# A whole-network kernel: the router's top two from one comparison of all pairs, and another order at the experts' end

## The chip, the cores and the metric

The kernel runs on 1 core of one Trainium2 chip. The metric is the device time in microseconds of one execution. The kernel before takes 2173.37 us, the median of 3 runs (2173.23 to 2174.28).

A core has TensorE (PE, matmuls, with its weight loads shown as PEld), VectorE (DVE), ScalarE (ACT), GpSimd (POOL), and SyncE (SP), from which most DMAs are issued here. Each engine works through its own instructions in the order in which they were written down, and waits on semaphores for the others.

## The reference

256 tokens of width 1024 go through two blocks. The first has two layers of SwiGLU, a token mixer of three attentions, and SwiGLU. The second has two layers of attention followed by a mixture of experts; this is the part that the change touches:

```python
def second_block(x, c, ...):
    silu_c = jax.nn.silu(c)
    for i in range(DEPTH):                                  # 2
        mod = silu_c @ ada_w[i] + ada_b[i]
        sh1, sc1, g1, sh2, sc2, g2 = [m[:, None, :] for m in jnp.split(mod, 6, axis=-1)]
        h = rms_norm_2(x, norm_mix_g[i]) * (1.0 + sc1) + sh1
        y = diff_attention(h, ...) if i % 2 == 0 else chunked_attention(h, ...)
        x = x + g1 * y
        h = rms_norm_2(x, norm_ffn_g[i]) * (1.0 + sc2) + sh2
        x = x + g2 * grouped_moe(h, router_w, router_bias, moe_w_gate[i], moe_w_up[i], moe_w_down[i])
    return x

def grouped_moe(h, router_w, router_bias, w_gate, w_up, w_down):
    scores = jax.nn.sigmoid(t @ router_w)                   # t: 256 tokens; 16 experts
    sel = scores + router_bias
    grp = sel.reshape(-1, N_GROUPS, E_PER_GROUP)            # 4 groups of 4
    group_score = lax.top_k(grp, TOP_K)[0].sum(-1)          # the two best of each group
    _, g_idx = lax.top_k(group_score, TOPK_GROUPS)          # the best group
    masked = jnp.where(expert_mask, sel, NEG_INF)
    _, e_idx = lax.top_k(masked, TOP_K)                     # the two best experts in it
    w = jnp.take_along_axis(scores, e_idx, axis=1)
    w = w / jnp.sum(w, axis=-1, keepdims=True)
    for e in range(N_EXPERTS):
        he = jax.nn.silu(t @ w_gate[e]) * (t @ w_up[e])
        out = out + gates[:, e:e + 1] * (he @ w_down[e])
```

## The kernel before

The tokens lie in two tiles of 128 partitions, `x[:, t]`, and each is worked on in halves of 512 columns. The program is one straight sequence of ten stages: 0 to 5 are block one; 6 is the differential attention, 7 the experts, 8 the chunked attention, 9 the experts again.

**Weights.** All weights come as pieces of 128 x 1024 through one stream, issued on SP (L81) into a shared ring of slots; a piece can be loaded when a slot is free. Outside the experts every product is made in three matmuls (L332 to L334): ACT casts the piece into a high part `hi` (L122), DVE subtracts it from the piece for the low part `lo` (L127), and PE multiplies hi by hi, hi by lo and lo by hi. The experts' weights are used as they come, unsplit (L1592 gate and up, L1611 and L1672 down).

**The plan.** `plan` writes down the order in which the stream's pieces are used. Among a stage's weights it mixes the rows of the modulation matrices (ada items) that the next stages need. An ada item brings no matmul: DVE multiplies it into an accumulator `aacc` (L420, L422); the last of a group leads to sums by PE (L440), a copy `zs` by ACT (L442), transposes by PE, and two small DVE steps `mc` (L454, L456). Before, the ada items of a stage are spread over all its units from the first on. In the experts' stage 7 the first four units of stage 8 are already loaded (`EARLY`, `mine`).

**Steps at the side.** Small steps wait in a queue and are let out between matmuls by `tick`; `flush` in the attention's output projection (`proj_halves`) runs what is left, one after the other.

**Router** (`moe`, L1842 on). Squares on ACT, a mean and a power (`rpow`: DVE L554, POOL L557) give each tile's norm factor `r`; PE makes the logits from transposed raw `x` (L1876), and `z` (L1880) applies the factor to them. `norm` scales x to `xn` (DVE, L1884), `high` and `low` split `xn` for the gather (L1887, L1891). After the Sigmoid (L1939) DVE adds the bias (`sel`) and finds the top two of each group by two calls of `first_hit` of five steps each (L1567 to L1574) and a step that masks the first hit, then the best group by a third call. `eb` marks the two experts; PE makes prefix sums of it (L1963 on), which with an offset per expert (`pz`) give each token's two slots (`pc`, `slot`, `sl`). One-hot rows of the slots (L1982, L1983) are the matrices by which PE gathers the tokens for the first chunk of four experts (L1717); ACT and DVE scale what was gathered into `hg` (L1720, L1722), and the experts' matmuls begin.

**End of the experts** (`pairs` and `end`). When the last pair of experts is done, each half of `x` is updated (L1636), squared (L2051), and each tile gets its factor by `rpow`; `normed` (L594) scales tile 0, PE transposes it, and `trans` (L596 on) applies the modulation (`hf`, L616) and splits it into `hT` (L617, L610) for the first product of stage 8. `fills(2)` takes two pieces of the stream in this place, one behind each tile's factor.

**Stage 8** (`attn2`, L1358 on). Heads go in two groups; each makes q, k (normalised on DVE, `qs` L1350, transposed on PE, scaled on ACT, `qk` L1355) and v (copied by ACT, L1396). Softmax units: scores on PE (L850, L853), bias and maximum on DVE (L872, L876), eight exponentials on ACT (L879), normalised (L887, L890), transposed on PE, multiplied by v (L913). They run between the projections' matmuls.

Of the kernel before, what the change touches and what calls it, by code (L numbers as in the profile page):

```python
# [21 lines left out]
P = 128  # L22
# [23 lines left out]
for _name, _w in (  # L46
    ("cc", 16), ("adab", 144), ("npre", 48), ("gpost", 48), ("adab2", 96), ("nmix", 16), ("nffn", 16),
    ("aqg", 1), ("akg", 1), ("bqg", 1), ("bkg", 1), ("subln", 1), ("router", 128), ("rbias", 16),
    ("cosp", 32), ("sinp", 32), ("cosm", 64), ("sinm", 64), ("code", 4), ("eoff", 32), ("coff", 4),
):  # L50
    CV[_name] = (_n, _w)
    _n += _w
# [135 lines left out]
class Net:  # L188
# [309 lines left out]
    def plan(self, stages):  # L498
# [23 lines left out]
        for st in stages:  # L522
            wl, mine, early = wls[st], early, []

            nxt = self.next.get(st)
            ahead = {len(wl) - 4 * (EARLY - i): wls[nxt][i] for i in range(EARLY)} if st > 6 and st % 2 and nxt else {}
            if st == stages[0]:
                k = 4 if st == 0 else 0
                for it in wl[:k] + first[n:]:
                    self.stream.add(*it)  # L530
                wl = wl[k:]
            must = sum(1 for s, late, _ in queue if s == st or (s == st + 1 and not late))
            n = max(must, min(len(queue), ADA_PER[st]))
            al, queue = queue[:n], queue[n:]
            span = ADA_SPAN[st] * len(wl)
            done = 0
            for i, it in enumerate(wl):
                while done < n and done * span <= i * n:
                    self.stream.add(*al[done][2])
                    done += 1  # L540
                if i in ahead:
                    early.append(self.stream.add(*ahead[i], later=True))
                if i < len(mine):
                    self.stream.uses.append(mine[i])
                else:
                    self.stream.add(*it)
            assert done == n
# [1029 lines left out]
    def pairs(self, hg, gsl, row, OHT, ahead, done, end):  # L1577
# [111 lines left out]
        fill = self.stream.fills(2)  # L1689
# [6 lines left out]
        end(0, 1, fill[:1])  # L1696
        end(1, 0)
        S(7, 1, 1)
        for f in fill[1:]:
            f()  # L1700
# [142 lines left out]
    def moe(self, st, pre, rest):  # L1843
# [42 lines left out]
        def high(t, q):  # L1886
            nc.scalar.copy(xs[0, t][:, q * 512:(q + 1) * 512], xn[t, q])  # L1887
# [39 lines left out]
        power(1)  # L1927
        low(0, 0)
# [33 lines left out]
        pp = self.ps("acc")
        nc.tensor.matmul(pp[:, 0:16], self.ustrictb, eb[:, :16], start=True, stop=True)  # L1963
        nc.tensor.matmul(pp[:, 16:32], self.ustrictb, eb[:, 16:], start=True, stop=False)
        nc.tensor.matmul(pp[:, 16:32], self.onesb, eb[:, :16], start=False, stop=True)
        nc.tensor.matmul(pp[:, 32:48], self.onesb, eb[:, :16], start=True, stop=False)
        nc.tensor.matmul(pp[:, 32:48], self.onesb, eb[:, 16:], start=False, stop=True)
        low(1, 0)
        pz = self.sm(32, name="pz", bufs=1)
        nc.vector.tensor_tensor(out=pz, in0=pp[:, :32], in1=self.col("eoff"), op=ALU.add)  # L1970
        pc = self.sm(64, name="pc", bufs=1)
        nc.vector.tensor_tensor(out=pc.rearrange("p (c n) -> p c n", c=2), in0=ch.rearrange("p (c n) -> p c n", c=2),
                                in1=pz[:, None, :].broadcast_to([P, 2, 32]), op=ALU.mult)
# [4 lines left out]
        nc.vector.tensor_tensor(out=v3(sl, 4), in0=slot[:, None, :].broadcast_to([P, 4, 4]), in1=self.col("coff")[:, :, None].broadcast_to([P, 4, 4]), op=ALU.subtract)  # L1978

        def hot(oh, t, c):  # L1980
            o = self.t2(name="oh1")
            nc.vector.tensor_scalar(out=o[:, :256], in0=self.iota, scalar1=sl[:, 4 * c + t:4 * c + t + 1], scalar2=None, op0=ALU.is_equal)  # L1982
            nc.vector.scalar_tensor_tensor(out=oh[:, t * 256:(t + 1) * 256], in0=self.iota, scalar=sl[:, 4 * c + 2 + t:4 * c + 3 + t], in1=o[:, :256],  # L1983
                                           op0=ALU.is_equal, op1=ALU.add)
# [4 lines left out]
        next(chunks[0])  # L1989
        low(1, 1)  # L1990
# [51 lines left out]
        def end(t, h, fills=()):  # L2042
# [20 lines left out]
        return nxt, lambda n: lambda: nxt and self.normed(nxt, 1, rs[1])  # L2063
# [19 lines left out]
def prep(inputs):  # L2083
# [7 lines left out]
    def tables(n_rot):  # L2091
# [16 lines left out]
        "eoff": rep(np.tile(1024 * np.arange(16), 2).astype(np.float32)), "coff": rep(4096 * np.arange(4).astype(np.float32)),  # L2108
    }
# [66 lines left out]
```

## Time and profile before

| | before |
|---|---|
| median of 3 runs | 2173.37 us (2173.23 to 2174.28) |
| the profiled execution | 2171.94 us, its span 2170.2 us |
| PE, DVE, ACT, POOL busy | 94%, 63%, 42%, 4% of the span |
| HBM read | 590.00 MB, 273 GB/s over the span |
| stages 6 to 9 end near | 1530, 1787, 1922, 2170 us |

The profiled execution is one of its own; its span is what the views show, and the 1.74 us around it are outside them. All durations in the rows are from it. A busy share is a mean over stages that have different limits: where a stage waits for weights, the DMA share is near 1 and PE's matmuls (0.60 us in the experts) follow the stream; where it doesn't, the gaps in PE's row count. A row of the timeline gives the start in us from the span's start, the duration, engine, line, operation, output and inputs, and in brackets how long the engine stood idle before it and what ended that.

### The profile page before, as it was taken

To read this page: it belongs to the slowest core of one execution; us is meant where nothing else is said; L and a number is where in the kernel's file an instruction comes from. 1 tells how busy PE (TensorE), PEld (TensorE's weight loads), DVE (VectorE), ACT (ScalarE), POOL (GpSimd) and SP (SyncE) were. 2 spreads that over 40 slices of the span, in tenths; PEclk is the share of its full clock that TensorE was granted. 3 is DMA by queue.
4 is the path that set the end of the run, shared out by engine and by line. 5 is a ranking of instruction groups with operands and counts; after the bars stand their busy time and mean duration, and the time that the engine had idled before them with its cause. 6 is when DMAs were issued, how large, how long until landed. Compare 5 with 4: busy or idle time off the path is not lost. (4 is left out here: it accounts for less than half of the span.)

```text
span 2170.2 us, 27088 instructions
## 1 busy us (share of the span) xinstructions
PE 2050.8 (94%) x9858; PEld 1437.9 (66%) x9858; DVE 1363.1 (63%) x2108; ACT 917.4 (42%) x1635; POOL 89.6 (4%) x118
## 2 busy tenths in 40 slices
PE   7999999988999999999989899998899989989998
PEld 4888777766888788777767688776533337763333
DVE  4976877558965886687647886697422258742223
ACT  3544454555544544355465544464211026621110
POOL 1000001000000000000000000030000002000000
PEclk9999999989999999999999999999899999989999
DMA  9987686527886787676635687666699996759998
GB/s 390 325 286 239 238 293 236 171 82 250 321 300 211 253 321 251 217 265 213 239 115 197 248 311 253 217 225 231 238 419 419 384 409 190 256 201 419 419 386 329
DMA packets 166956, 595.08 MB, mean 274 GB/s; under 512 B 18744, under 2 KB 18832, under 8 KB 166816
## 3 DMA queue, kind: packets, MB, share of 16 engines
q1 hardware_dynamic: 162864, 582.16, 72.8%
q0 software_dynamic: 2064, 6.88, 1.2%
q10 hardware_dynamic: 1888, 4.24, 0.6%
q8 instruction: 80, 1.31, 0.2%
q14 instruction: 60, 0.49, 0.1%
HBM read 590.00 MB, written 3.20 MB: 273 GB/s over the span
## 5 line engine op out<-in xcount | busy, mean ns | idle before, releaser
L127 DVE TENSOR_TENSOR lo<-raw,hi 128x1024 fp32r<-128x1024 f32 x478 | 570.3, 1214 | 37.0 <-ACT hi L122 35.5
L332 PE MATMUL psw<-hi,hT 128*128 128x512 f32 (+1 forms) x1296 | 525.8, 406 | 10.4 <-ACT hT L617 9.6
L334 PE MATMUL psw<-lo,hT 128*128 128x512 f32 (+1 forms) x1296 | 507.8, 392 | 5.9 <-DVE lo L127 5.8
L333 PE MATMUL psw<-hi,hT 128*128 128x512 f32 (+1 forms) x1296 | 507.6, 392 | 0.0
L122 ACT CAST hi<-raw 128x1024 fp32r<-128x1024 f32 x478 | 479.1, 1047 | 51.0 <-DMA raw<-in_w_gu_dram 16.9
L332 PEld LDWEIGHTS psw<-hi,hT 128*128 128x128 f32 x1296 | 244.7, 189 | 75.5 <-ACT hT L617 13.5
L334 PEld LDWEIGHTS psw<-lo,hT 128*128 128x128 f32 x1296 | 244.5, 189 | 59.6 <-DVE lo L127 8.5
L333 PEld LDWEIGHTS psw<-hi,hT 128*128 128x128 f32 x1296 | 245.2, 189 | 46.2
L422 DVE SCALAR_TENSOR_TENSOR aacc<-raw,csil,aacc 128x1024 f32<-128x1024 f32 x196 | 250.5, 1278 | 0.0
L1592 PE MATMUL psw<-raw,hg 128*64 128x512 f32 x1024 | 238.7, 605 | 5.7 <-PEq L2024 3.8
L1592 PEld LDWEIGHTS psw<-raw,hg 128*64 128x64 f32 x1024 | 69.0, 138 | 131.4 <-issue 122.5
L332 PE MATMUL psacc<-hi,gT 128*128 128x512 f32 x352 | 139.9, 397 | 6.0 <-ACT gT L725 3.1
L334 PE MATMUL psacc<-lo,gT 128*128 128x512 f32 x352 | 138.8, 394 | 1.0 <-DVE lo L127 1.0
L333 PE MATMUL psacc<-hi,gT 128*128 128x512 f32 x352 | 139.0, 395 | 0.0
L1636 DVE TENSOR_TENSOR x<-x,psacc 128x512 f32<-128x512 f32 x64 | 43.0, 686 | 121.3 <-PE psacc L1632 121.3
L1611 PE MATMUL psacc<-raw,gT 128*64 128x512 f32 x448 | 104.7, 598 | 0.4 <-DMA raw<-in_moe_d_dram 0.4
L688 ACT ACTIVATE sg<-psw 128x256 f32<-128x256 f32 x86 | 32.7, 384 | 153.9 <-PE psw L334 152.5
L557 POOL TENSOR_TENSOR r<-m,nhalf 128x1 f32<-128x1 f32 (+3 forms) x30 | 45.4, 1512 | 1218.1 <-DVE m L554 815.1
L689 DVE TENSOR_TENSOR sg<-psw,sg 128x256 f32<-128x256 f32 x86 | 35.9, 422 | 92.8 <-ACT sg L688 92.7
L725 ACT CAST gT<-psw 128x256 fp32r<-128x256 f32 x88 | 29.5, 375 | 130.0 <-PE psw L383 130.0
L332 PEld LDWEIGHTS psacc<-hi,gT 128*128 128x128 f32 x352 | 66.9, 190 | 22.1 <-ACT gT L725 4.8
L334 PEld LDWEIGHTS psacc<-lo,gT 128*128 128x128 f32 x352 | 66.9, 190 | 15.8 <-DVE lo L127 1.9
(331 smaller groups left out, 2314.1 us busy)
## 6 DMA issues: line engine op xcount, KB each, us to landing
raw<-in_ada_dram SPq DMA_DIRECT2D x224, 512.0 KB, 4.8
raw<-in_w_gu_dram SPq DMA_DIRECT2D x176, 512.0 KB, 4.9
raw<-in_moe_g_dram SPq DMA_DIRECT2D x128, 512.0 KB, 9.9
raw<-in_moe_u_dram SPq DMA_DIRECT2D x128, 512.0 KB, 9.9
raw<-in_moe_d_dram SPq DMA_DIRECT2D x128, 512.0 KB, 9.9
raw<-in_w_mix_dram SPq DMA_DIRECT2D x96, 512.0 KB, 4.6
raw<-in_w_dn_dram SPq DMA_DIRECT2D x88, 512.0 KB, 4.6
raw<-in_w_qkv_dram SPq DMA_DIRECT2D x48, 512.0 KB, 4.8
```

Of the source, the lines that this page charges most:

```text
L122: nc.scalar.copy(hi[:, :cols], raw[:, :cols])
L127: nc.vector.tensor_tensor(out=lo[:, :cols], in0=raw[:, :cols], in1=hi.bitcast(F32)[:, :cols], op=ALU.subtract)
L332: mm(ps, a[0], w[0], start=first, stop=False)
L333: mm(ps, a[1], w[0], start=False, stop=False)
L334: mm(ps, a[0], w[1], start=False, stop=last)
L422: nc.vector.scalar_tensor_tensor(out=acc, in0=raw, scalar=c, in1=acc, op0=ALU.mult, op1=ALU.add)
L557: nc.gpsimd.tensor_tensor(out=r, in0=m, in1=self.nhalf[:, :w], op=ALU.pow)
L688: nc.scalar.activation(sg[:, :256], ps[:, :256], AF.Silu)
L689: nc.vector.tensor_tensor(out=sg[:, 256:], in0=ps[:, 256:], in1=sg[:, :256], op=ALU.mult)
L1592: mm(ps[s], hg(k, j)[:, s], w[0][:, i * 512:(i + 1) * 512], start=k == 0, stop=k == KC - 1)
L1611: mm(yb[h][s], gT[:, f * P + s.start:f * P + s.stop], w[0][:, h * 512:(h + 1) * 512], start=f == 0, stop=f == 3)
L1636: nc.vector.tensor_tensor(out=self.x[:, t, s], in0=self.x[:, t, s], in1=ps, op=ALU.add)
```

## The change

Five things are changed.

1. *Top two.* Instead of two calls of `first_hit` for the experts, one step compares all pairs within a group (`ge`, 128 elements), a second masks it with a constant, a third subtracts its transpose, and a sum gives each expert a place. `top` (place among the first two), `s2` and the group score follow; `first_hit` stays for the group. `eb` is `top` times the group's mark. What tells the first from the second expert (`first`, `ch`) comes after `eb`. The offsets are added by PE to the prefix sums (a matmul of `ident` with `eoff`), so that `pz` goes; chunk 0 uses `slot` itself, and `sl` is made later.
2. *Norms of the second tile* are made by ACT, after the Sigmoid; `scores(0)` stands ahead of `low(0, 0)`; three of the four `low` steps stand behind chunk 0's one-hots.
3. *Experts' end.* There is no `fills(2)`, and tile 1's factor (`power2(1)`) is made where `rest(4)` is called in stage 8, which is after tile 0's transposes.
4. *Plan.* Ada items start only behind the units that are already loaded. This moves something in stage 8 alone.
5. The constants grow from 765 to 789 columns.

```diff
@@ plan
-                while done < n and done * span <= i * n:
+                while done < n and done * span <= max(i - len(mine), 0) * n and i >= len(mine):
                     self.stream.add(*al[done][2])
@@ pairs
-        fill = self.stream.fills(2)
...
-        end(0, 1, fill[:1])
+        end(0, 1)
         end(1, 0)
         S(7, 1, 1)
-        for f in fill[1:]:
-            f()
         end(1, 1)
@@ moe: norms
         power(1)
+        scores(0)
         low(0, 0)
         high(0, 1)
         nc.scalar.activation(sc[:, :1], self.half, AF.Sigmoid)
         logits(1, 0)
         logits(1, 1)
-        for q in range(2):
-            norm(1, q)
-            high(1, q)
-        scores(0)
-        low(0, 1)
         scores(1)
         nc.scalar.activation(sc, z, AF.Sigmoid)
+        for q in range(2):
+            xn[1, q] = self.t2(name="xn")
+            nc.scalar.activation(xn[1, q], self.x[:, 1, q * 512:(q + 1) * 512], AF.Copy, scale=r[1])
+            high(1, q)
@@ moe: choice
-        m1, o1 = self.first_hit(sv, 8, 4)
+        nc.vector.tensor_tensor(out=ge, in0=sv[:, :, None, :].broadcast_to(by), in1=sv[:, :, :, None].broadcast_to(by), op=ALU.is_ge)
+        nc.vector.tensor_tensor(out=ge, in0=ge, in1=self.col("earlier")..., op=ALU.mult)
+        nc.vector.tensor_tensor(out=df, in0=ge, in1=ge.rearrange("p n i j -> p n j i"), op=ALU.subtract)
+        nc.vector.tensor_reduce(out=place, in_=df, axis=AX.X, op=ALU.add)
+        nc.vector.tensor_tensor(out=top, in0=place, in1=at(1), op=ALU.is_le)
-        nc.vector.scalar_tensor_tensor(out=s2, in0=o1, scalar=NEG, in1=sv, op0=ALU.mult, op1=ALU.add)
-        m2, o2 = self.first_hit(s2, 8, 4)
+        nc.vector.tensor_tensor(out=s2, in0=top, in1=sv, op=ALU.mult)
-        nc.vector.tensor_tensor(out=gsc, in0=m1, in1=m2, op=ALU.add)
+        nc.vector.tensor_reduce(out=gsc, in_=s2, axis=AX.X, op=ALU.add)
         _, goh = self.first_hit(gsc.rearrange("p (t g) -> p t g", t=2), 2, 4)
+        nc.vector.tensor_tensor(out=o, in0=top, in1=g, op=ALU.mult)          # eb
+        nc.tensor.matmul(pp[:, 0:32], self.ident, self.col("eoff"), start=True, stop=False, ...)
...
+        nc.vector.tensor_tensor(out=ch[:, 32:], in0=eb, in1=ch[:, :32], op=ALU.subtract)
-        low(1, 0)
-        nc.vector.tensor_tensor(out=pz, in0=pp[:, :32], in1=self.col("eoff"), op=ALU.add)
...
         next(chunks[0])
+        low(1, 0)
+        low(0, 1)
         low(1, 1)
@@ moe: end
+        def power2(t):
+            v = self.sm(1, name="v")
+            nc.vector.tensor_tensor(out=v, in0=ns[t][:, 0:1], in1=ns[t][:, 1:2], op=ALU.add)
+            self.rpow(v, D, r=rs[t])
...
-                self.rpow(v, D, r=rs[t])
-                for f in fills:
-                    f()
-                if t == 0:
-                    self.normed(nxt, 0, rs[0])
+            if h and t == 0:
+                power2(0)
+                self.normed(nxt, 0, rs[0])
...
+        def rest(n):
+            if nxt:
+                power2(1)
+            return lambda: nxt and self.normed(nxt, 1, rs[1])
```

Where the order on an engine changes, three places are shown.

DVE in the router of stage 7, before, from the last split ahead of the second `z` to the second search (`fm`, `fo`, `fn`, `fr` are `first_hit`'s):

```order
L1891 TENSOR_TENSOR xs_13342<-xn_13373,xs_13341 128x512
L1880 SCALAR_TENSOR_TENSOR z_13286<-psw_13363,rx_13395,sw_13147 128x16
L1941 TENSOR_TENSOR sel_13420<-sc_13287,cv 128x32
L1567 TENSOR_REDUCE fm_13422<-sel_13420 128x8
L1569 TENSOR_TENSOR fo_13424<-sel_13420,fm_13422 128x32
L1570 TENSOR_TENSOR fo_13424<-fo_13424,cv 128x32
L1572 TENSOR_REDUCE fn_13427<-fo_13424 128x8
L1574 TENSOR_TENSOR fr_13429<-cv,fn_13427 128x32
L1947 SCALAR_TENSOR_TENSOR s_13431<-fr_13429,sel_13420 128x32
L1567 TENSOR_REDUCE fm_13433<-s_13431 128x8
L1569 TENSOR_TENSOR fo_13435<-s_13431,fm_13433 128x32
```

And after, from the first `z` on:

```order
L1877 SCALAR_TENSOR_TENSOR z_13286<-psw_13362,rx_13300,sw_13147 128x16
L1888 TENSOR_TENSOR xs_13342<-xn_13371,xs_13341 128x512
L1877 SCALAR_TENSOR_TENSOR z_13286<-psw_13363,rx_13395,sw_13147 128x16
L1938 TENSOR_TENSOR sel_13419<-sc_13287,cv 128x32
L1946 TENSOR_TENSOR ge_13421<-sel_13419 128x128
L1947 TENSOR_TENSOR ge_13421<-ge_13421,cv 128x128
L1949 TENSOR_TENSOR ge_13421<-ge_13421 128x128
L1951 TENSOR_REDUCE place_13425<-ge_13421 128x32
L1954 TENSOR_TENSOR top_13427<-place_13425,cv 128x32
L1957 TENSOR_TENSOR s_13429<-top_13427,sel_13419 128x32
L1959 TENSOR_REDUCE gsc_13431<-s_13429 128x8
L1567 TENSOR_REDUCE fm_13433<-gsc_13431 128x2
```

The first `z` and the split stand one behind the other ahead of the second `z`, no `xn` is left there, and seven steps lead from `sel` to the group scores in place of twelve.

DVE at the end of stage 7, before, from tile 0's factor (`v`, `m`) to the first `hf` of stage 8 (`gq` is a constant of stage 8):

```order
L2054 TENSOR_TENSOR v_15099<-ss_15090 128x1
L554 TENSOR_SCALAR m_15101<-v_15099 128x1
L422 SCALAR_TENSOR_TENSOR aacc_12458<-raw_14990,csil,aacc_12458 128x1024
L594 TENSOR_SCALAR xn_15105<-x,rx_13553 128x512
L594 TENSOR_SCALAR xn_15106<-x,rx_13553 128x512
L1636 TENSOR_TENSOR x<-x,psacc_15112 128x512
L422 SCALAR_TENSOR_TENSOR aacc_12458<-raw_15004,csil,aacc_12458 128x1024
L2054 TENSOR_TENSOR v_15118<-ss_15109 128x1
L554 TENSOR_SCALAR m_15120<-v_15118 128x1
L1364 TENSOR_SCALAR gq_15123<-cv 128x1
L616 TENSOR_SCALAR hf_15139<-psw_15129,mc_152,mc_151 128x128 x2
```

And after:

```order
L2058 TENSOR_TENSOR v_15090<-ss_15081 128x1
L554 TENSOR_SCALAR m_15092<-v_15090 128x1
L594 TENSOR_SCALAR xn_15095<-x,rx_13544 128x512
L594 TENSOR_SCALAR xn_15096<-x,rx_13544 128x512
L1636 TENSOR_TENSOR x<-x,psacc_15102 128x512
L1364 TENSOR_SCALAR gq_15107<-cv 128x1
L616 TENSOR_SCALAR hf_15123<-psw_15113,mc_152,mc_151 128x128 x2
L610 TENSOR_TENSOR hT_15111<-hf_15123,hT_15109 128x128
```

The two products `aacc` and tile 1's `v` and `m` are gone from it; they follow behind the last `hT`.

ACT in the middle of stage 8, before (`sb` with x4 twice are the eight exponentials of the first softmax unit, `qk` the scaled transposes, `v` the copies):

```order
L442 COPY zs_15569<-psw_15564 128x256
L879 ACT_TABLE_LOAD
L879 ACTIVATE sb_15590,rs_15577<-sb_15590,mx_15592 128x128 x4
L879 ACTIVATE sb_15598,rs_15577<-sb_15598,mx_15600 128x128 x4
L122 CAST hi_15609<-raw_15555 128x1024
L122 CAST hi_15618<-raw_15613 128x1024
L122 CAST hi_15645<-raw_15640 128x1024
L1355 ACTIVATE qk_15427<-psw_15656,gq_15123 128x4x128
L122 CAST hi_15667<-raw_15665 128x1024
L1355 ACTIVATE qk_15427<-psw_15674,gq_15123 128x4x128
L1396 COPY v_15537<-psw_15538 128x512
L1396 COPY v_15537<-psw_15539 128x512
```

And after:

```order
L122 CAST hi_15575<-raw_15566 128x1024
L122 CAST hi_15594<-raw_15568 128x1024
L122 CAST hi_15601<-raw_15570 128x1024
L1355 ACTIVATE qk_15415<-psw_15605,gq_15107 128x4x128
L122 CAST hi_15629<-raw_15624 128x1024
L879 ACT_TABLE_LOAD
L879 ACTIVATE sb_15646,rs_15633<-sb_15646,mx_15648 128x128 x4
L879 ACTIVATE sb_15654,rs_15633<-sb_15654,mx_15656 128x128 x4
L1396 COPY v_15525<-psw_15526 128x512
L1396 COPY v_15525<-psw_15527 128x512
L1355 ACTIVATE qk_15415<-psw_15676,gq_15107 128x4x128
```

The second of the two `qk` and the copies of `v` now stand behind the eight exponentials.

## Rows read from the trace of the kernel before

**Rows 1.** Windows: stretch, length, busy PE, PEld, DVE, ACT, POOL; granted clock, DMA share, GB/s.

```profile
1540.00:1550.00 10.00, 4.80 (x26) 4.47 (x25) 7.13 (x28) 0.95 (x2) 0.00 (x0) 0.52 0.00 1
...
1560.00:1570.00 10.00, 10.00 (x56) 4.80 (x54) 1.63 (x3) 1.69 (x3) 0.00 (x0) 1.00 1.03 420
...
1800.00:1850.00 50.00, 46.51 (x229) 35.62 (x227) 36.92 (x56) 30.33 (x58) 14.17 (x9) 0.97 0.69 211
```

**Rows 2.** Timeline, router of stage 7: start, duration, engine, line, idle before it.

```profile
1534.38 2.21 PE L1876 MATMUL psw<-gw,xT 128*128 128x16 f32 x16
...
1536.58 0.88 DVE L1884 TENSOR_SCALAR xn<-x,rx 128x512 f32<-128x512 f32 x2 [0.45 <-POOL rx L557]
...
1538.12 0.23 DVE L1880 SCALAR_TENSOR_TENSOR z<-psw,rx,sw 128x16 f32<-128x16 f32 x1
...
1538.71 0.19 DVE L1941 TENSOR_TENSOR sel<-sc,cv 128x32 f32<-128x32 f32 x1 [0.36 <-ACT sc L1939]
...
1542.79 0.19 DVE L1961 TENSOR_TENSOR eb<-ch 128x32 bf16<-128x32 f32 x1
...
1545.46 6.13 PE L1717 MATMUL psw<-OH,xs 128*128 128x256 f32 x32 [2.15 <-DVE OH L1983]
...
1551.52 0.65 PE L1592 MATMUL psw<-raw,hg 128*64 128x512 f32 x2
```

**Rows 3.** Timeline, DVE in stage 6: two rows on 128 elements.

```profile
1511.35 0.28 DVE L1302 TENSOR_TENSOR gw<-cv,mc 128x128 f32<-128x128 f32 x1
...
1511.87 0.37 DVE L1305 TENSOR_REDUCE sw<-sw 128x16 f32<-128x128 f32 x1
```

**Rows 4.** Timeline, the router of stage 9.

```profile
1923.82 2.50 PE L1876 MATMUL psw<-gw,xT 128*128 128x16 f32 x16
...
1928.14 0.19 DVE L1941 TENSOR_TENSOR sel<-sc,cv 128x32 f32<-128x32 f32 x1 [0.35 <-ACT sc L1939]
```

**Rows 5.** Timeline, end of stage 7 and start of stage 8.

```profile
1782.54 1.28 DVE L422 SCALAR_TENSOR_TENSOR aacc<-raw,csil,aacc 128x1024 f32<-128x1024 f32 x1
1782.70 1.52 POOL L557 TENSOR_TENSOR rx<-m,nhalf 128x1 f32<-128x1 f32 x1 [246.15 <-DVE m L554]
...
1784.80 1.61 PE L383 MATMUL psw<-ident,xn 128*128 128x128 f32 x8 [3.18 <-DVE xn L594]
...
1787.16 0.72 DVE L616 TENSOR_SCALAR hf<-psw,mc,mc 128x128 f32<-128x128 f32 x2
1787.27 0.55 POOL L557 TENSOR_TENSOR rx<-m,nhalf 128x1 f32<-128x1 f32 x1 [3.04 <-DVE gq L1364]
...
1787.95 0.79 PE L332 MATMUL psw<-hi,hT 128*128 128x512 f32 x1 [1.54 <-ACT hT L617]
```

**Rows 6.** Timeline, middle of stage 8: PE and ACT.

```profile
1834.10 0.58 PE L332 MATMUL psw<-hi,hT 128*128 128x512 f32 x1
...
1838.43 0.39 ACT L879 ACTIVATE sb<-sb,mx 128x128 f32<-128x128 f32 x1
...
1842.13 0.63 PE L383 MATMUL psw<-ident,qs 128*128 128x128 f32 x4 [1.98 <-DVE qs L1350]
...
1845.07 1.08 PE L383 MATMUL psw<-ident,qs 128*128 128x128 f32 x4 [0.25 <-DVE qs L1350]
...
1846.74 0.40 PE L334 MATMUL psw<-lo,hT 128*128 128x512 f32 x1
1846.78 1.07 ACT L1396 COPY v<-psw 128x512 f32<-128x512 f32 x2
...
1894.99 1.94 PE L383 MATMUL psw<-ident,sb 128*128 128x128 f32 x8 [3.82 <-DVE sb L890]
...
1899.38 0.63 PE L333 MATMUL psacc<-hi,yT 128*128 128x512 f32 x1
```

**Rows 7.** Timeline, the modulation row of stage 8 on ACT.

```profile
1877.34 0.37 ACT L442 COPY zs<-psw 128x256 f32<-128x256 f32 x1 [0.81 <-PE psw L440]
```

**Rows 8.** The page, part 5: the low halves' matmuls over the whole program.

```profile
L334 PE MATMUL psw<-lo,hT 128*128 128x512 f32 (+1 forms) x1296 | 507.8, 392 | 5.9 <-DVE lo L127 5.8
```

More of the change, by code (lines that the diff above doesn't have):

```diff
@@ L48 @@
     ("aqg", 1), ("akg", 1), ("bqg", 1), ("bkg", 1), ("subln", 1), ("router", 128), ("rbias", 16),
-    ("cosp", 32), ("sinp", 32), ("cosm", 64), ("sinm", 64), ("code", 4), ("eoff", 32), ("coff", 4),
+    ("cosp", 32), ("sinp", 32), ("cosm", 64), ("sinm", 64), ("code", 4), ("eoff", 32), ("coff", 4), ("earlier", 16), ("place", 8),
 ):
@@ L1944, in moe @@
         sv = sel.rearrange("p (n e) -> p n e", n=8)
-        m1, o1 = self.first_hit(sv, 8, 4)
+        pair = self.t2(name="ge")
+        ge = pair[:, :128].rearrange("p (n i j) -> p n i j", n=8, i=4)
+        by = [P, 8, 4, 4]
+        nc.vector.tensor_tensor(out=ge, in0=sv[:, :, None, :].broadcast_to(by), in1=sv[:, :, :, None].broadcast_to(by), op=ALU.is_ge)
+        nc.vector.tensor_tensor(out=ge, in0=ge, in1=self.col("earlier").rearrange("p (i j) -> p i j", i=4)[:, None].broadcast_to(by), op=ALU.mult)
@@ new lines, in moe @@
+        df = pair[:, 128:256].rearrange("p (n i j) -> p n i j", n=8, i=4)
+        nc.vector.tensor_tensor(out=df, in0=ge, in1=ge.rearrange("p n i j -> p n j i"), op=ALU.subtract)
+        place = self.sm(32, name="place", bufs=1).rearrange("p (n e) -> p n e", n=8)
+        nc.vector.tensor_reduce(out=place, in_=df, axis=AX.X, op=ALU.add)
+        at = lambda c: self.col("place")[:, 4 * c:4 * c + 4][:, None, :].broadcast_to([P, 8, 4])
+        top = self.sm(32, name="top", bufs=1).rearrange("p (n e) -> p n e", n=8)
@@ L1962, in moe @@
[L1962 to L1967, printed above, removed]
-        low(1, 0)
-        pz = self.sm(32, name="pz", bufs=1)
@@ L1970, in moe @@
-        nc.vector.tensor_tensor(out=pz, in0=pp[:, :32], in1=self.col("eoff"), op=ALU.add)
+        of = lambda a: (a.rearrange("p (n e) -> p n e", n=8), goh.rearrange("p t g -> p (t g)")[:, :, None].broadcast_to([P, 8, 4]))
+        eb = self.sm(32, BF16, name="eb")
+        o, g = of(eb)
+        nc.vector.tensor_tensor(out=o, in0=top, in1=g, op=ALU.mult)
+        pp = self.ps("acc")
+        nc.tensor.matmul(pp[:, 0:32], self.ident, self.col("eoff"), start=True, stop=False, skip_group_check=True)
@@ new lines, in moe @@
+        for i, (a, w) in enumerate(((self.ustrictb, eb[:, :16]), (self.ustrictb, eb[:, 16:]), (self.onesb, eb[:, :16]))):
+            nc.tensor.matmul(pp[:, 16 * (i > 0):16 * (i > 0) + 16], a, w, start=False, stop=i != 1, skip_group_check=True)
+        nc.tensor.matmul(pp[:, 32:48], self.onesb, eb[:, :16], start=False, stop=False, skip_group_check=True)
+        nc.tensor.matmul(pp[:, 32:48], self.onesb, eb[:, 16:], start=False, stop=True, skip_group_check=True)
+        ch = self.sm(64, name="ch", bufs=1)
@@ L1971, in moe @@
+        first = self.sm(32, name="first", bufs=1)
+        nc.vector.tensor_tensor(out=first.rearrange("p (n e) -> p n e", n=8), in0=place, in1=at(0), op=ALU.is_equal)
+        o, g = of(ch[:, :32])
+        nc.vector.tensor_tensor(out=o, in0=first.rearrange("p (n e) -> p n e", n=8), in1=g, op=ALU.mult)
+        nc.vector.tensor_tensor(out=ch[:, 32:], in0=eb, in1=ch[:, :32], op=ALU.subtract)
+        q = self.sm(96, name="q6", bufs=1)
         pc = self.sm(64, name="pc", bufs=1)
         nc.vector.tensor_tensor(out=pc.rearrange("p (c n) -> p c n", c=2), in0=ch.rearrange("p (c n) -> p c n", c=2),
-                                in1=pz[:, None, :].broadcast_to([P, 2, 32]), op=ALU.mult)
+                                in1=pp[:, None, :32].broadcast_to([P, 2, 32]), op=ALU.mult)
@@ L1977, in moe @@
         sl = self.sm(16, name="sl", bufs=1)
-        nc.vector.tensor_tensor(out=v3(sl, 4), in0=slot[:, None, :].broadcast_to([P, 4, 4]), in1=self.col("coff")[:, :, None].broadcast_to([P, 4, 4]), op=ALU.subtract)
         def hot(oh, t, c):
+            a = (lambda i: slot[:, i:i + 1]) if c == 0 else (lambda i: sl[:, 4 * c + i:4 * c + i + 1])
             o = self.t2(name="oh1")
-            nc.vector.tensor_scalar(out=o[:, :256], in0=self.iota, scalar1=sl[:, 4 * c + t:4 * c + t + 1], scalar2=None, op0=ALU.is_equal)
-            nc.vector.scalar_tensor_tensor(out=oh[:, t * 256:(t + 1) * 256], in0=self.iota, scalar=sl[:, 4 * c + 2 + t:4 * c + 3 + t], in1=o[:, :256],
+            nc.vector.tensor_scalar(out=o[:, :256], in0=self.iota, scalar1=a(t), scalar2=None, op0=ALU.is_equal)
+            nc.vector.scalar_tensor_tensor(out=oh[:, t * 256:(t + 1) * 256], in0=self.iota, scalar=a(2 + t), in1=o[:, :256],
                                            op0=ALU.is_equal, op1=ALU.add)
@@ L1996, in moe @@
             nc.scalar.dma_start(xd[t][:, i * 512:(i + 1) * 512], a)
-        nc.vector.tensor_copy(q[:, :32], pp[:, :32])
+        nc.vector.tensor_tensor(out=v3(sl, 4), in0=slot[:, None, :].broadcast_to([P, 4, 4]), in1=self.col("coff")[:, :, None].broadcast_to([P, 4, 4]), op=ALU.subtract)
+        nc.vector.tensor_tensor(out=q[:, :32], in0=pp[:, :32], in1=self.col("eoff"), op=ALU.subtract)
         big = self.sm(16, name="big")
         nc.vector.tensor_copy(big, pp[:, 32:48])
-        nc.vector.tensor_tensor(out=q[:, 32:64], in0=ch[:, :32], in1=ch[:, 32:], op=ALU.add)
+        nc.vector.tensor_copy(q[:, 32:64], eb)
         gz = q[:, 64:96]
@@ L2040, in moe, with end @@
         ns = {}
-        def end(t, h, fills=()):
+        def power2(t):
+            v = self.sm(1, name="v")
+            nc.vector.tensor_tensor(out=v, in0=ns[t][:, 0:1], in1=ns[t][:, 1:2], op=ALU.add)
+            self.rpow(v, D, r=rs[t])
+        def end(t, h):
             s = slice(h * 512, (h + 1) * 512)
@@ L2108, in prep @@
         "eoff": rep(np.tile(1024 * np.arange(16), 2).astype(np.float32)), "coff": rep(4096 * np.arange(4).astype(np.float32)),
+        "earlier": rep(np.tril(np.ones((4, 4), np.float32), -1).reshape(16)), "place": rep(np.concatenate([np.arange(-3, 1), np.arange(-2, 2)]).astype(np.float32)),
     }
```

10 lines of the change are left out of this document (1 added, 9 removed).

## The prediction

> **What bounds the kernel now.** I read the windows by stretch first, because the change touches few places and the question is which of them the end follows. In the router of stage 7 the DMA engines stand still (share 0.00 from 1540 to 1550) and TensorE has its lower clock for much of the time (0.52 granted); twenty microseconds later the DMA share is 1.03 at 420 GB/s [rows 1]. So the experts run at the rate of the weight stream, and the stream restarts only when the first expert matmul (L1592, 1551.52) begins to free slots. What the router saves is therefore saved at the end of the stage, one for one. Stage 9 has the same router, and from it the stream runs to the end of the program.
>
> Next the timeline of that router: one chain, Sigmoid, choice, prefix sums, one-hots, gather [rows 2]. Then the stage after the experts, stage 8: from 1800 to 1850 PE is busy 46.51 of 50 us, DVE 36.92 and the DMA share is 0.69 [rows 1]. There PE sets the time, and the rows to look for are those in which PE stands idle, and how fast its matmuls are afterwards [rows 5, 6]. The time of a stretch there is work plus idle time plus what the clock takes.
>
> **The change part by part.** *Router, up to `sel`.* Before, the second factor (POOL, in time for `xn` at 1536.58) releases two scalings (0.88), a `z` and a split, and then the last `z` at 1538.12; `sel` follows it by 0.59 [rows 2]. After, the scalings are on ACT behind the Sigmoid and the first `z` and split are done earlier, so the last `z` waits only for the factor and for the logits, which end at 1534.38 + 2.21 = 1536.59. It starts near 1536.65, `sel` at 1537.24: gain 1.47. In stage 9 the logits end at 1923.82 + 2.50 = 1926.32, `sel` near 1926.96 in place of 1928.14: 1.18 [rows 4]. ACT's two scalings per router cost nothing, since ACT has nothing else to do until the gather.
>
> *From `sel` to `eb`.* Before 1542.79 - 1538.71 = 4.08 for 20 steps, 0.204 each [rows 2]. After, 13 steps. Three have 128 elements and one sums 128: rows of that size take 0.28 and 0.37 [rows 3], with the 0.03 that lies between dependent steps 0.31 and 0.40. Nine stay small, five of them on 8 elements. Together 3 x 0.31 + 0.40 + 9 x 0.204 = 3.2: gain 0.9. No row shows a pattern of four dimensions with a repeated operand. If that costs as much again as the plain one, 1.3 more, the gain turns into -0.4; if the four cost no more than small steps, it is 1.4. I take the rows' own price.
>
> *From `eb` to the gather.* 1545.46 - 1542.79 = 2.67. `pc` comes after three small DVE steps (`eb` and these, 4 x 0.215 = 0.86, while PE does the prefix sums) where it came after a split and `pz`, 0.93; the shift `sl` goes, 0.25 with its gap: 0.3 gained. The fourth gather matmul now waits for a split of 0.68 behind the one-hots, 0.4 later. About -0.1 (bounds -0.5 to 0.3). Per router 2.3 and 2.0: **4.3** (1.5 to 5.8 for both).
>
> *End of the experts.* At 1782.54 a product (`aacc`, 1.28) starts on DVE, and the POOL power beside it takes 1.52 to 1784.22; the next one, beside other work, 0.55 [rows 5]. The scaling `xn`, the transposes and the first matmul at 1787.95 hang on it. Without the product I take 0.55 for the power, 0.97 earlier. The second product and the two steps of tile 1's power stand ahead of `hf` too: the transposes end at 1784.80 + 1.61 = 1786.4, `hf` starts at 1787.16, 0.7 later than it could, and with them gone it follows the transposes. Together **1.7**: the first matmul at about 1786.25. Bounds: 0.7 (the power is no faster) to 3.0 (PE's clock also comes back earlier, as its idle time shrinks).
>
> The Trainium skill ("SBUF — State Buffer", Who interferes with whom) says a DVE instruction with two SBUF inputs and a POOL one that reads SBUF exclude each other, the later waiting for the earlier to end. By that rule the power began after the product's end at 1783.82, which the row bears out, and the 0.97 is sure; if the durations of POOL's rows were only scatter, that term would be nothing.
>
> *Middle of stage 8.* The plan puts the modulation work behind the four early units, which shifts units against the first group's softmax. Before, PE waits 1.98 and 0.25 for `qs` around 1842, and from 1842.13 to 1846.74 eight matmuls and eight transposes that would take 2.6 take 4.4 at the lower clock: 4.0 lost [rows 6]. After, the second transposes of `qs` need a PSUM buffer that a copy of `v` frees, and this copy stands on ACT behind eight exponentials. From the scores' end (matmuls behind them start at 1834.10) to the end of the eighth exponential and one copy is 1838.43 + 0.39 + 0.54 - 1834.10 = 5.26; six matmuls of PE (1.4) lie in it. So PE idles about 3.8 in one piece. At full clock afterwards that is +0.2; with the drop seen at 1842 (1.8) -1.6; with that behind the 3.82 of idle time at 1894.99, where eight transposes take 1.94 and the matmuls after them 0.63 where 0.40 is usual (3.1 lost in all), -2.9. I take **-1.6**, since the same instructions follow as in this place before.
>
> The Trainium skill ("TensorE: Matmul & The Clock Gate", Why this matters for your kernels) warns that an idle gap between bursts puts TensorE back to the lower clock. By that page the gap costs the drop as well, and the sum is the one with -2.9; both gaps in the rows above agree, with matmuls and transposes slow behind them.
>
> *Rest of stage 8.* Six matmuls move into the idle 3.82 before 1894.99 [rows 6]: +1.4, bounds 0 to 2.0. A split gets ahead of the last softmax unit on DVE: -0.3. The row's sums, transposes and final transpose, hidden among other PE work before, run back to back in the flush, and PE waits for the `zs` copy (0.37 with some 0.15 to and from it) and for the two small steps on DVE (0.4, two of rows 2's pitch): -0.9, bounds -1.5 to -0.3 [rows 7]. The constants grow by 12 KB: -0.1.
>
> Sum: 4.3 + 1.7 - 1.6 + 1.4 - 0.3 - 0.9 - 0.1 = **4.5** gained. The profiled execution took 2171.94 (span 2170.2 and 1.74 around it), 1.43 under the median 2173.37. It would become 2167.4; moved to the median, **2168.9**.
>
> **The rivals.** *B, stage 8 gives it back.* The long wait behind the exponentials drops the clock for as long as at 1894.99, the six matmuls bring nothing because another wait takes that place, and the flush costs 1.5: 4.3 + 1.7 - 2.9 - 0.3 - 1.5 - 0.1 = 1.2 gained, **2172.2**. For it: both gaps of rows 6 are followed by slow matmuls. Against: the six moved ones do fill a stretch that is idle now.
>
> *C, slower: DVE becomes the bound of stage 8.* Ten products of 1.28 that stood partly in PE's idle edge now stand between the splits from the fifth unit on. If the splits have less than 1.28 of lead there, each makes PE wait: 12.8 lost against 4.3 + 1.7 - 0.1 = 5.9, so 6.9 net, **2180.3**. Against: PE waited for the low halves (L334 from DVE L127) 5.8 us in 1296 matmuls [rows 8], and DVE was idle 13 of 50 us in rows 1's stretch. It decides as soon as a split ends later than the high half's two matmuls.
>
> *D, the router isn't on the path*, because the stream refills anyway or the pair comparison is no shorter: 4.3 less, gain 0.2, **2173.2**. Against: the 0.00 share.
>
> *G, the clock stays up* behind the one long wait, and the head of stage 8 gets its clock earlier (2.5 of its 3.0): 4.3 + 2.5 + 0.2 + 1.4 - 0.3 - 0.9 - 0.1 = 7.1, **2166.3**. For it: behind 1842 the full rate was back by 1846.74. Against: rows 6, as for B.
>
> **How the numbers follow.** Forecast 0.50, its own range 2167 to 2171; G 0.20, B 0.11, D 0.08, C 0.11. 0.2% of the median is 4.35, about what can be told from no change, so faster means under 2169.0 and slower over 2177.7. The forecast's centre lies close to that bound: 0.28 of its 0.50 counts as faster, 0.22 as the same. With G faster is 0.48, with B and D the same is 0.41, and C is slower, 0.11. The range reaches from below G (its terms with the router at its upper bound, 1.5 more: 2164.8) to just above D, 2173.6; C is left out.
>
> **What would show it.** Right: in the new trace `sel` comes about 1.4 earlier than before relative to the end of the logits, `eb` follows it by 3.2, the gather `eb` by 2.4; the power at the end of the experts takes 0.55; the second transposes of `qs` wait once, near 3.8, with an ACT copy of `v` as the cause; the flush holds three short PE waits. Wrong: `ge` over 0.45, a DMA share above 0.1 in the router, waits of L334 above 12 us in the whole (C), or a start of the gather that is earlier by 4 us in both routers while the end doesn't move (D).

## The result and the profile after

The kernel after takes 2186.26 us (median of 6, 2183.73 to 2190.19) against 2174.89 us of the kernel before in the same sessions (6 runs, 2173.23 to 2177.83). The ratio is 1.0054, 95% interval 1.0044 to 1.0065: about 11.8 us slower, where 4.5 us faster were forecast. The profiled execution took 2183.84 us, its span 2181.8.

The first view to compare is the windows. This is a stretch of stage 7, away from every router, in the kernel before and then in the kernel after (stretch, length, busy PE, PEld, DVE, ACT, POOL, granted clock, DMA share, GB/s):

```profile
1600.00:1700.00 100.00, 100.00 (x470) 38.87 (x468) 28.79 (x52) 13.11 (x23) 0.00 (x0) 1.00 1.03 419
1600.00:1700.00 100.00, 100.00 (x467) 38.40 (x464) 28.38 (x49) 13.11 (x23) 0.00 (x0) 1.00 1.03 409
```

The DMA share is 1.03 in both, and yet only 409 GB/s arrive where 419 did. The DMA engines are as busy as before and bring less. The experts' stages read 192 pieces of 512 KB each, 100.7 MB: 240 us at 419 GB/s and 246 us at 409. Twice 6 us are as much as the whole loss, in a stretch where not one instruction was changed.

The router, timeline of the kernel after (it answers to [rows 2]):

```profile
1538.13 2.01 PE L1873 MATMUL psw<-gw,xT 128*128 128x16 f32 x16
...
1541.06 0.19 DVE L1938 TENSOR_TENSOR sel<-sc,cv 128x32 f32<-128x32 f32 x1 [0.35 <-ACT sc L1932]
1541.29 0.29 DVE L1946 TENSOR_TENSOR ge<-sel 128x128 f32<-128x128 f32 x1
...
1541.94 0.39 DVE L1949 TENSOR_TENSOR ge<-ge 128x128 f32<-128x128 f32 x1
1542.36 0.29 DVE L1951 TENSOR_REDUCE place<-ge 128x32 f32<-128x128 f32 x1
...
1544.35 0.19 DVE L1966 TENSOR_TENSOR eb<-top,fr 128x32 bf16<-128x32 f32 x1
...
1546.73 6.05 PE L1714 MATMUL psw<-OH,xs 128*128 128x256 f32 x32 [1.85 <-DVE OH L1994]
```

From the logits' start to the gather it is 8.60 us, before 1545.46 - 1534.38 = 11.08 [rows 2]: 2.5 gained. The pair steps cost 0.29, with the transposed operand 0.39.

The experts' end and stage 8 (answering to [rows 5, 6]; the 5.05 has no row before):

```profile
1789.50 0.55 POOL L557 TENSOR_TENSOR rx<-m,nhalf 128x1 f32<-128x1 f32 x1 [249.07 <-DVE m L554]
...
1790.63 1.09 PE L383 MATMUL psw<-ident,xn 128*128 128x128 f32 x8 [2.21 <-DVE xn L594]
...
1792.62 0.73 PE L332 MATMUL psw<-hi,hT 128*128 128x512 f32 x1 [0.90 <-ACT hT L617]
...
1851.21 1.11 PE L383 MATMUL psw<-ident,qs 128*128 128x128 f32 x4 [3.59 <-ACT v L1396]
...
1901.22 0.79 PE L334 MATMUL psacc<-lo,yT 128*128 128x512 f32 x1 [5.05 <-DVE lo L127]
1901.82 0.63 PE L332 MATMUL psacc<-hi,yT 128*128 128x512 f32 x1
```

The power takes the 0.55 that was expected, the transposes of `qs` wait 3.59 for a copy of `v`, and where PE waited 3.82 for the softmax before [rows 6], it now waits 5.05 for a low half, with matmuls of 0.63 behind it in place of 0.40.

### The profile page after: what moved, and what is told of

It is laid out like the page before. It is cut to its first block, busy times and chain, and to the rows that moved or that the text cites. A ratio compares the mean times of both kernels' runs of the same rounds, so it can differ in the third digit from the quotient of the medians.

```text
span 2181.8 us, 27093 instructions
## 1 busy us (share of the span) xinstructions
PE 2061.2 (94%) x9862; PEld 1441.7 (66%) x9862; DVE 1360.4 (62%) x2094; ACT 919.6 (42%) x1639; POOL 88.9 (4%) x118
## 5 line engine op out<-in xcount | busy, mean ns | idle before, releaser
L332 PE MATMUL psw<-hi,hT 128*128 128x512 f32 (+1 forms) x1296 | 526.1, 406 | 10.7 <-ACT hT L617 8.9
L334 PE MATMUL psw<-lo,hT 128*128 128x512 f32 (+1 forms) x1296 | 508.1, 392 | 5.8 <-DVE lo L127 5.8
L332 PEld LDWEIGHTS psw<-hi,hT 128*128 128x128 f32 x1296 | 244.9, 189 | 75.7 <-ACT hT L617 12.7
L334 PEld LDWEIGHTS psw<-lo,hT 128*128 128x128 f32 x1296 | 244.6, 189 | 60.3 <-DVE lo L127 8.8
L332 PE MATMUL psacc<-hi,gT 128*128 128x512 f32 x352 | 140.8, 400 | 6.0 <-ACT gT L725 3.1
L334 PE MATMUL psacc<-lo,gT 128*128 128x512 f32 x352 | 139.5, 396 | 0.6 <-DVE lo L127 0.5
L332 PEld LDWEIGHTS psacc<-hi,gT 128*128 128x128 f32 x352 | 67.1, 191 | 22.0 <-ACT gT L725 4.8
L334 PEld LDWEIGHTS psacc<-lo,gT 128*128 128x128 f32 x352 | 67.2, 191 | 15.7 <-DVE lo L127 1.7
```

What stands on the lines that cost most here:

```text
L332: mm(ps, a[0], w[0], start=first, stop=False)
L334: mm(ps, a[0], w[1], start=False, stop=last)
```

## The experiments

What else differs between the two programs is where things lie. The constants' tile is allocated ahead of the 38 weight slots; 24 more columns are 96 bytes per partition, and every slot begins 96 bytes higher: the first one at byte 34144 of its partition, which is 96 past a multiple of 256, where it was at 34048, a multiple of 256. That this place costs the time was theory 1; that the new order costs it was theory 2.

| kernel | slots past a multiple of 256 | GB/s, 1600 to 1700 | ratio to before (95%) |
|---|---|---|---|
| after | 96 | 409 | 1.0054 (1.0044 to 1.0065) |
| e1: before, 24 columns more | 96 | 409 | 1.0068 (1.0055 to 1.0081) |
| e2: after, 8 columns more | 128 | 409 | 1.0056 (1.0043 to 1.0069) |
| e3: before, 32 columns more | 128 | 409 | 1.0056 (1.0043 to 1.0069) |
| e4: router alone | 128 | 409 | 1.0036 (1.0023 to 1.0049) |
| f1: before, gap of 128 bytes | 128 | 409 | 1.0063 (1.0046 to 1.0080) |
| f2: before, larger input only | 0 | 419 | 0.9996 (0.9987 to 1.0006) |
| f3: before, gap of 256 bytes | 0 | 419 | one run, 2173.97 us |
| g3: before, gap of 64 bytes | 64 | 409 | one run, 2187.75 us |
| f4: after, gap of 416 bytes | 0 | 419 | 0.9999 (0.9989 to 1.0008) |
| g1: router alone | 0 | 419 | 0.9981 (0.9972 to 0.9990) |
| g2: router and experts' end | 0 | 419 | 0.9982 (0.9973 to 0.9991) |
| h1: all, plan in part | 0 | 419 | 0.9994 (0.9985 to 1.0003) |

**Where the slots lie.** These edits are to the constants or behind them only (in e2, e4, f4, g1, g2 and h1 on the changed kernel; what else e4, g1, g2 and h1 change stands with them below):

```diff
 e1, e3 (24, 32), e2, e4 (8)
+    cv["pad"] = rep(np.zeros(24, np.float32))       # and ("pad", 24) in the list of columns
 f1, f3, g3 (32, 64, 16), f4, g1, g2, h1 (104)
         self.cv = c([P, CV_N], F32, name="cv")
+        self.gap = c([P, 32], F32, name="gap")
 f2
-        nc.sync.dma_start(self.cv, ins["cv"])
+        nc.sync.dma_start(self.cv, ins["cv"][:, :CV_N])        # the input itself is 797 wide
```

e1: 

> The kernel before, with 24 unused columns behind its constants: no instruction moves, the constants are 789 columns wide as in the kernel after, and all buffers behind them (the 38 weight slots among them) begin 96 bytes higher, 32 bytes past a multiple of 64. Theory 1 (addresses): the transfers run at about 409 GB/s in the experts instead of 419, and the ratio to the kernel before is 1.0065 (3.75 us lost by the first router, as the traces of before and after differ there, and 2.4% of about 225 us in each of the experts' stages). Theory 2 (the new order in stage 8 and at the experts' end costs the time, rival C and the like): ratio 1.000, 419 GB/s.

e3: 

> The kernel before with 32 unused columns (797): more bytes of constants than the kernel after has, but the slots at a multiple of 64. Theory 1: ratio 1.000, 419 GB/s. Theory 3 (it is the size of the constants, their transfer or the room they take, not where the slots begin): ratio 1.006 or more, as for 24 columns.

e2: 

> The kernel after, with 8 more unused columns (797), so that the weight slots begin 128 bytes higher than in the kernel before, at a multiple of 64. Theory 1: 419 GB/s again, ratio about 0.9985 (the routers' gain of some 2.3 each stays, stage 8 gives a part back). Theory 2: ratio 1.0054 as for the kernel after, 409 GB/s or a longer stage 8 whatever the address.

e1 is the kernel before with wider constants, to the last instruction the same, and takes 1.0068 of its time: all that the change lost and more. That finishes theory 2 as the main cause. e3 and e2, though, were to be fast by theory 1 as it stood, which asked for a multiple of 64, and both run at 409. So either the multiple was wrong or it is the size or the HBM side.

f1: 

> The kernel before with an unused tile of 128 bytes per partition behind the constants: the constants, their input and their transfer stay at 765 columns, only what is allocated behind them on the chip begins 128 bytes higher, as with 32 more columns. If the place of the slots on the chip sets the rate (a multiple of 256 is lost): 409 GB/s in the experts, ratio about 1.006. If it is where the weights lie in HBM behind a larger input: 419 GB/s, ratio 1.000.

f2: 

> The kernel before with the input of constants 797 columns wide in HBM, of which the same 765 are loaded: nothing moves on the chip, only the input is larger (and its rows are read with a stride). If the place of the slots on the chip sets the rate: 419 GB/s, ratio 1.000. If it is where the weights lie in HBM: 409 GB/s, ratio about 1.006.

f3: 

> The kernel before with an unused tile of 256 bytes behind the constants, so that the slots begin at a multiple of 256 again, and of 512, where before it was 256 past one. If the place on the chip decides and a multiple of 256 is what is wanted: 419 GB/s. If it must be 256 past a multiple of 512, or any shift is harmful: 409 GB/s. If HBM decides: 419 GB/s.

g3: 

> The kernel before with an unused tile of 64 bytes behind the constants: slots 64 past a multiple of 256. If any shift off a multiple of 256 lowers the rate: 409 GB/s in the experts. If a multiple of 64 that is not 128 past is enough: 419 GB/s.

The windows of f1:

```profile
1600.00:1700.00 100.00, 100.00 (x468) 38.37 (x466) 29.08 (x51) 13.73 (x24) 0.00 (x0) 1.00 1.03 409
```

and of f2:

```profile
1600.00:1700.00 100.00, 100.00 (x466) 38.33 (x464) 28.70 (x50) 13.11 (x23) 0.00 (x0) 1.00 1.03 419
```

An unused tile behind unchanged constants costs what the change cost; a larger input costs nothing. f3 is fast and g3 slow (one run each, and their windows show the two rates): slots 64, 96 or 128 bytes past a multiple of 256 give 409, a multiple of 256 gives 419, be it a multiple of 512 (f3) or not. The sixteen smaller buffers that lie behind the slots move with them, and no run moves the slots alone; but the weight stream, whose rate is what changed, writes into nothing else.

The Trainium skill ("DMA: Bandwidth & Descriptors", How a descriptor splits into AXI transactions) says that a transfer goes in transactions of at most 256 bytes which must start at a multiple of 256, so that one that starts past a multiple has to begin at the boundary below, and the bytes fetched there for nothing cost time too. It says so of reads; here it is the written side that was shifted. By its count of 32-byte beats a row of 4096 bytes shifted by 64, 96 or 128 bytes would take 130, 131 or 132 beats in place of 128, an estimate of 1.6, 2.3 or 3.1% more. The measured 2.4% agree with that in direction and about in size, but not in the grading, since all three shifts give the same 409. Nor is every row longer: by the records of single transfers of 4096 bytes between 1600 and 1700, nearly every one takes 159 ns in before and f4, while in after, e3 and g3 they take 159 to 172 ns, 163 in the mean, and a fifth to a third of them still 159.

**The order by itself.** f4: 

> The kernel after with an unused tile of 416 bytes behind its 789 columns, so that the slots begin 512 bytes higher than in the kernel before (same place within 512). If the place on the chip decides: 419 GB/s, and the order of the change is seen by itself: with the router's 4.3 us gained (as the router alone showed against the kernel before at the slower rate) and about as much given back, ratio 0.998 to 1.000. If HBM decides: 409 GB/s and 1.0055 as for the kernel after.

With the slots at a multiple of 256 the whole change comes out even, 0.9999. Where its gain goes is seen by stretches, all from the timelines of PE: from the start of the last 16 logits matmuls in stage 7 to the first L332 of stage 8, from there to the same logits in stage 9, and from those to the end of the span.

| us | logits 7 to stage 8 | stage 8 to logits 9 | logits 9 to the end |
|---|---|---|---|
| before | 253.57 | 135.87 | 246.38 |
| f2 (before's order) | 253.61 | 136.14 | 244.95 |
| f4 (all) | 248.57 | 142.65 | 244.16 |
| g1 (router) | 251.33 | 135.21 | 244.17 |
| g2 (router, end) | 249.95 | 136.52 | 244.38 |
| h1 (all, plan in part) | 249.16 | 140.86 | 244.72 |
| e3 (before's order, 409 GB/s) | 260.43 | 136.23 | 252.33 |
| after (all, 409 GB/s) | 254.49 | 139.52 | 249.66 |
| e2 (all, 409 GB/s) | 254.28 | 140.29 | 250.87 |

e3 shows the rate's price again, 6.8 and 6 to 7.4. f4 gains 5.0 up to stage 8 and loses 6.6 in it. It is the dearest of the three traces of this order: after and e2 lose 3.5 and 4.3 in stage 8, which the rate hardly touches (e3 136.23). The longest waits of PE there, from f4's view of waits (us in total, times, longest):

```profile
PE psacc L335 <- DVE lo L127: 5.1, 1, 5.1
PE psw L384 <- ACT v L1397: 3.6, 1, 3.6
```

(A gap tile moves f4's lines by one: L335 is L334.) DVE in front of the first of them, f4's timeline:

```profile
1889.21 1.28 DVE L423 SCALAR_TENSOR_TENSOR aacc<-raw,csil,aacc 128x1024 f32<-128x1024 f32 x1
...
1893.24 1.29 DVE L891 TENSOR_TENSOR sb<-sb,rs 128x512 f32<-128x512 f32 x2
1894.45 1.22 DVE L127 TENSOR_TENSOR lo<-raw,hi 128x1024 fp32r<-128x1024 f32 x1
```

and the kernel before in the same place:

```profile
1888.96 1.29 DVE L890 TENSOR_TENSOR sb<-sb,rs 128x512 f32<-128x512 f32 x2
1890.17 1.22 DVE L127 TENSOR_TENSOR lo<-raw,hi 128x1024 fp32r<-128x1024 f32 x1
```

A product of the modulation now has the place that a split had, and the split comes a softmax unit later, at 1894.45 where 1889.21 was its turn, 5.2 us. PE has done the two high matmuls of the next piece and stops at the third. The matmuls behind it take 0.63 where 0.40 is usual, as in [rows 6].

The other loss stands at the stage's end. DVE's first step on the finished projection, and SP, in f4:

```profile
1906.58 4.76 SPq L81 DMA_DIRECT2D raw<-in_moe_g_dram  x6
1911.43 0.70 SPq L477 DMA_DIRECT2D row<-rowd  x1
...
1920.58 0.69 DVE L1290 TENSOR_TENSOR res<-psacc,row 128x512 f32<-128x512 f32 x1 [6.98 <-DMA row<-rowd]
```

Six pieces of the experts' weights go out within 4.76 us just ahead of the modulation row, and it lands after PE is done. In the order of before the same pieces stand ahead of it, but further apart; from f2:

```profile
1895.59 15.09 SPq L81 DMA_DIRECT2D raw<-in_moe_g_dram  x6
...
1917.22 0.69 DVE L1289 TENSOR_TENSOR res<-psacc,row 128x512 f32<-128x512 f32 x1 [5.77 <-DMA row<-rowd]
```

There too the row can be what comes last, but hardly later than PE: in f2 the logits of stage 9 start 18.29 us after the last multiplication by v (1907.86 to 1926.15), in before, where that step waited for PE, 18.28 (1905.54 to 1923.82). In f4 it is 21.93 (1906.71 to 1928.64). Of the 3.65 more the flush is 1.95 (from 1910.60, one pitch of 0.23 behind the matmul at 1910.37, to 1912.55: 1.2 of PE's own work, which stood earlier in the stage before, and waits of 0.49 and 0.26); the other 1.7 I put down to the late row. No run tests that by itself, and in after and e2 what is left beside the flush is 0.4 and 1.1, so this price changes with when the row lands.

e4: 

> The router's part of the change alone (pair comparison, second tile's norms on ACT, order of the low parts), with the plan and the experts' end as before, 797 columns of constants, the slots at a multiple of 64. Theory 1 with the prediction's router term: 4.3 us less than before, ratio 0.998. If the router isn't on the path: 1.000. If the changed router itself slows the experts' stream: above 1.002.

g1: 

> The router's part of the change alone (plan and experts' end as before), with the slots 512 bytes higher than in the kernel before, at a multiple of 256. Theory (the address sets the stream's rate, the router gains 2.3 and 2.0, stage 8 gave it back by the new plan): 419 GB/s, ratio 0.998 (4.3 us faster). Rival (the router's gain is swallowed by something in the stages behind it, and the 4.3 seen between the two kernels at the slower rate was scatter): 1.000.

```diff
 e4, g1 (the changed kernel with)
+                while done < n and done * span <= i * n:
+        fill = self.stream.fills(2)
+                for f in fills:
+                    f()
 ...                                                 # end and rest as before
```

The router alone gains 0.0019 of the time, 4.1 us, with the slots in order, and 0.0020 against e3 at the slower rate. It is on the path at either rate. The rival is out.

g2: 

> The router's part and the experts' end of the change, with the plan of before, slots at a multiple of 256. Theory (the plan puts a product ahead of a split behind the last softmax unit, 5.05 of idle time where there were 3.82, and sends the row's transfer behind six pieces of the experts' weights; without the plan both are gone): 0.9975 or lower, the router's 4.3 and 1.5 to 2 from the experts' end; the trace has no wait of 5 us for a low half, and the row is there before its use. Rival (the experts' end, not the plan, costs the time in stage 8, since the two products come later): 0.9995 to 1.000, and the wait of 5 us stays.

```diff
 g2 (the changed kernel with)
-                while done < n and done * span <= max(i - len(mine), 0) * n and i >= len(mine):
+                while done < n and done * span <= i * n:
```

Without the new plan the wait of 5.05 is gone, the logits follow the last multiplication by v by 18.28 again, and stage 8 is back to 136.52. That far the theory held. The experts' end brings 1.4 before stage 8 (251.33 to 249.95), but stage 8 returns 1.3, since its first low halves now wait behind products, 1.55 and, 3.7 later, 0.27; the first from g2's timeline of PE:

```profile
1795.24 0.50 PE L335 MATMUL psw<-lo,hT 128*128 128x512 f32 x1 [1.55 <-DVE lo L127]
```

So the ratio is that of the router alone, not 0.9975.

h1: 

> The whole change with slots at a multiple of 256, but of the plan only its first part: the modulation rows start behind the four early units and then follow one by one until they stand where the plan of before has them. On DVE no product stands then between the last softmax units (they are followed by a split each). Theory (a product that takes a split's place there is what gave 5.05 of idle time and, with the row behind the experts' weights, most of what stage 8 lost): no wait of 5 us for a low half, ratio 0.9970 to 0.9980, at or below the kernel with the plan of before (0.9982), since the low halves at the stage's start no longer wait behind products (1.55 and 0.27 there). Rival (what the new plan costs is the wait for the copies of v behind eight exponentials in the middle of the stage, and its lower clock): that wait of 3.6 stays here too, and the ratio is 0.999 to 1.000.

```diff
 h1 (the changed kernel with)
-                while done < n and done * span <= max(i - len(mine), 0) * n and i >= len(mine):
+                while done < n and done * span <= (i if i > len(mine) else 0) * n and i >= len(mine):
```

Here the theory fell, and what the rival forecast came: the wait of 5 us for a low half is gone, but the one for the copies of `v` is 3.6 as in f4, and the ratio is 0.9994. That wait isn't the whole of it, since the last softmax waits are longer than in [rows 6] as well (4.57 and 1.44; before 3.82 and 0.28). Taking the product away from behind the last unit isn't enough: other waits have grown. Stage 8 takes 140.86.

g1 and g2 are the best versions, faster than both kernels; they can't be told apart.

## Why the prediction was wrong

It failed at the smallest term of its sum, "The constants grow by 12 KB: -0.1". That priced the bytes. The 96 bytes per partition moved all weight slots off a multiple of 256, and such a move costs 12 to 15 us (e3, f1, e1). No rival had it, and the range ended below it.

With that taken out (f4) the change should have gained 4.5 and gained 0.2. Step by step:

- *Router*: right. 2.5 and, in stage 9, from logits to gather 9.30 (1932.14 to 1941.44) in place of 11.07, 1.8; predicted 2.3 and 2.0. In the other traces with the new router the second gain lies between 1.3 (f4, e2) and 2.5 (e4). `sel` to `eb` took 3.29 (3.2 predicted), `eb` to the gather 2.38 (2.4). Against the end of the logits `sel` came 0.3 later than worked out: the last `z` waits for the power, which took 1.08 us in place of 0.94, beside a split again. Rival D is out by g1.
- *Experts' end*: the size was right in its place (the power 0.55; 1.4 earlier in g2, 2.7 in f4 against g1, predicted 1.7). What was missing is the product's new place, which in g2 gives the 1.4 back.
- *Middle of stage 8*: the wait was worked out as 3.8 and measured 3.59, but the term was too small. From the first matmul to the last scores (1888.15 before, 1887.18 in f4) f4 took 1.0 longer, though six matmuls (1.4) and the flush's 1.2 had left this part: 3.6 lost, 1.6 predicted. Longer waits are 2.2 of it: 6.0 in all (the 3.59 among them, and 0.78 and 0.26 where the first softmax meets the projection) against 3.8 (1.98 and 0.25 among them). Another 1.0 is the clock at the stage's head: the first two stretches of 5 us were granted 0.50 (the lower level, 1.2 GHz, all through) and 0.89 in f4, 0.59 and 1.00 before, so 5 x (0.09 + 0.11) us of full clock are missing. That part belongs to f4's trace and not to the order, for after and e2 were granted 0.66 and 1.00 there, and this part took them 100.1 where f4 took 101.2: they lost 2.5.
- *"Six matmuls move into the idle 3.82: +1.4"* and *"-0.3"* for the split: wrong in sign. They did move, 21 matmuls of the output projection stand now between the last scores and the last multiplication by v where there were 15, but beside the idle time, not in it: 19.53 us in place of 17.39. I counted matmuls into a gap without asking whether their split was ready. DVE is the engine that the gap waits for, so a split that stands behind the softmax on it can't be.
- *Flush* -0.9: waits of 0.75, right. What the late row costs (1.7 in f4) wasn't in the sum. I had looked at the row that is written there, which stage 9 uses, but not at how close ahead of the one that is read the plan puts the experts' pieces in SP's queue.

Rival C had the mechanism, a product ahead of a split that is due, but as a price on every product. It struck once, for 5.05 us, where the split missed not one product's 1.28 but a softmax unit. The total of the waits for low halves [rows 8] is 5.8 in the kernel after too: the one that mattered stands in another row, that of the output projection.

What stays open: what the late row costs by itself, the last 0.3 to 0.4 of the middle of stage 8, and why 64, 96 and 128 bytes give one and the same rate.

## What to carry to other kernels

Before pricing a change, compare where the buffers of the large transfers begin, not only the instructions; a few more columns in a tile that is allocated ahead of them move them all, and padding them to a multiple of 256 bytes cost no time here (f3). If the DMA share stays at its ceiling and the GB/s fall, look there first. And a gap can only be filled by work whose inputs are not themselves still to come from the engine that the gap waits for.

## What the runs showed of the hardware that was not expected

- Where the stream is the bound, transfers of 512 KB into slots that begin 64, 96 or 128 bytes past a multiple of 256 run at 409 GB/s, at a multiple of 256 at 419, with the same DMA share of 1.03 (e1, e3, f1, g3 against f2, f3, f4). The single transfers of 4096 bytes take 163 ns in the mean in place of 159.
- The start of the router in stage 7, after stages whose instructions are the same in all kernels, scatters from 1534.38 to 1538.59 at 419 GB/s (seven traces, mean 1536.9) and from 1537.55 to 1541.26 at 409 (seven, mean 1538.7). So of the 3.75 between the first two traces, which e1's expectation took as an effect, about 1.8 go with the rate, and the rest is scatter.
- The POOL power on one column took 0.55 with DVE idle (1789.50 in the kernel after) and also beside `hf`, which DVE reads from PSUM; beside a split it took 0.94 and 1.08, beside a product 1.52 [rows 5]. In the kernel after it ended 0.42 behind the split beside it.
